# Second projection of a hybrid decoder block: copies and weight steps pinned, lag of three products, another order at its end

## The chip, the core and the metric

The kernel runs on one core of a Trainium2 chip. Its engines work in parallel, each through its own stream of instructions: TensorE (PE in the profile; its weight loads are PEld), VectorE (DVE), ScalarE (ACT), GpSimd (POOL) and SyncE (SP), from whose queue the DMA transfers leave. The metric is the device time of one execution in microseconds (us), the median of several runs.

## The reference

One decoder layer on 1024 tokens of width 1024, in float32. Two mixers read the same normalised input; each is projected, the two are merged by gates, and an output projection and a residual add follow:

```python
o_r = (head_groupnorm(o_r, ret_gn_g[l], ret_gn_b[l]) * jax.nn.silu(gr.astype(jnp.float32))).astype(x.dtype)
y = jax.nn.sigmoid(gate_a) * (o_a @ w_proj_a[l]) + jax.nn.sigmoid(gate_b) * (o_r @ w_proj_b[l])
x = x + y @ w_out[l]
xn2 = rmsnorm(x, norm2_g[l])
x = x + jnp.square(jax.nn.relu(xn2 @ w_up[l])) @ w_down[l]
```

The change concerns `o_r @ w_proj_b`, the second projection: 2048 inputs to 1024 outputs for 1024 tokens, with the gate and the sum that make `y`, up to the start of `y @ w_out`.

## The kernel before

**Arithmetic.** Every float32 operand is split into a high and a low part (`split`, L349 to L353): ScalarE copies the high part (L350), VectorE subtracts it for the low part (L353). A product of two operands is then three matmuls, high by high, high by low and low by high. The large products are also done by a seven-product scheme (Strassen in Winograd's form): a unit of 256 outputs has the products N1 to N7, and each product is 4 x 3 = 12 matmuls.

**Second projection** (from L1130). There are eight units, 0 to 3 for the first half of the inputs and 4 to 7 for the second; `order` (L1131 to L1135) lists the 56 products. Unit j runs N6, N5, N7, N4, N3, and in between N1 and N2 of unit j + 2 are run ahead; the last ten entries are of units 6 and 7 alone: N6, N5, N7 of 6, N6 of 7, N4 of 6, N5 and N7 of 7, N3 of 6, N4 and N3 of 7. Products of one unit share three banks of PSUM (`BANK`, L280): N1 and N2 add into bank a, N6, N7 and N4 into bank b, N5 and N3 into bank d. Between two of them the bank is copied out by ScalarE: after N1 (L419, negated, into bank b), after N6 (L424) and after N7 (L427). The next product of that bank may not start before its copy is done.

**Results.** N2, N7, N4 and N3 each finish a result (`result`, L1156): a block of 128 outputs by 512 tokens. For units 0 to 3 it goes to memory (`pb_d`), for half of them after being gated. For units 4 to 7 it is added up, gated by the sigmoid of a gate loaded from `sg_d`, added to the first projection's block (L1171 to L1173 or L1175 and L1176, on VectorE) and split into the rows that the output projection reads (`keep`, L1151), either at once or, for the even lower halves, after a trip through memory (`yl_d`). Each result asks for the loads of the result after next (`fetch`) and runs the sigmoid of the next one (L906). The first gate's sigmoid is run ahead of the loop (L1196).

**Weights** (`Weights`, L38). A queue of weight steps is run in order by `pump`. A unit has two raw loads of 128 x 1024 on SP and four steps: A (for N1 and N2), D (for N4), then four sums of raw blocks (L124, on VectorE), B (for N6 and N3) and C (for N5 and N7). A step needs its raw block and the release of its weight buffer (`W.free` at the end of `product`). `lag` counts how many products must lie between the request of a load and a step on it; `tick`, once a product, runs at most one step. After the 32 steps of this stage come the eight of the output projection (`add`).

**Order.** TensorE's stream is the program's order. For the other engines a planner orders the instructions by when it thinks them ready, so an instruction may move ahead of others that stand before it in the program. `tc.keep_in_program_order` ties one instruction behind the one that was traced last on its engine. Before the change the sigmoids (L906) are tied so, and the splits of the operands at the end of the stage before (`part_sum`); in this stage bank copies, weight steps and results aren't.

Of the kernel before, what the change touches and what calls it, by code (L numbers as in the profile page):

```python
# [10 lines left out]
F = mybir.dt.float32  # L11
R = mybir.dt.float32r
AF = mybir.ActivationFunctionType
OP = mybir.AluOpType
# [23 lines left out]
class Weights:  # L38
# [10 lines left out]
    A, B, C, D = (0, 1), (2, 3), 5, 4  # L49
# [24 lines left out]
            self.last[p] = key  # L74
        return before

    def add(self, src, buf=None):

        n = self.plain
        if buf is None:  # L80
            buf = self.cycle[self.turn % self.WB]
            self.turn += 1
        r = len(self.src)
        self.src.append(src)
        self.place.append(n % self.RAW)
        w = src.shape[1]

        def step():
            h, l = self.buffer(buf)
            self.split(h[:, :w], l[:, :w], self.raw[r][:, :w])  # L90
            self.units[n] = h, l
            self.used.add(r)

        self.steps.append((self.claim(buf, n), r, step))
        self.plain += 1

    def add_units(self, tag, srcs, flip=0):

        base = len(self.src)
        self.first[tag] = len(self.steps)  # L100
        kept = {}
        for s in srcs:
            self.place += [(len(self.src) + i - base) % (self.RAW + 1) for i in range(2)]
            self.src += [s[1], s[0]]

        def piece(key, buf, r, cols, then=None):
            def step():
                if isinstance(buf, tuple):
                    if not kept:
                        kept["D"] = self.buffer(buf[0])  # L110
                    h, l = (x[:, 512 * buf[1]:512 * buf[1] + 512] for x in kept["D"])
                else:
                    h, l = self.buffer(buf)
                self.split(h, l, self.raw[r][:, cols], key[0] == "up" and key[1] < 2 and key[2] != "A")
                self.units[key] = h, l
                if then:
                    then()

            self.steps.append((self.claim(buf, key), r, step))

        def sums(r):
            (x22, x21), (x11, x12) = ((self.raw[i][:, 0:512], self.raw[i][:, 512:1024]) for i in (r, r - 1))
            for x, y in ((x22, x21), (x21, x11), (x11, x22), (x12, x11)):
                ins = self.nc.vector.tensor_tensor(x, x, y, op=OP.add)  # L124
                if tag == "up" and r <= base + 3:
                    self.keep(ins)

        both = slice(0, 1024)
        for j in range(-1, len(srcs)):
            if j + 1 < len(srcs):  # L130
                piece((tag, j + 1, "A"), self.A[(j + 1) % 2], base + 2 * (j + 1), both)
            if j >= 0:
                r = base + 2 * j + 1
                piece((tag, j, "D"), (self.D, j % 2), r, slice(0, 512), lambda r=r: sums(r))
                piece((tag, j, "B"), self.B[(j + flip) % 2], r - 1, both, lambda r=r: self.used.add(r - 1))
                piece((tag, j, "C"), self.C, r, both, lambda r=r: self.used.add(r))
        m = len(srcs) + flip
        self.cycle = (0, 1, self.B[m % 2], self.C, self.D, self.B[(m - 1) % 2])
        self.turn = 0
# [90 lines left out]
class Pipe:  # L230
# [22 lines left out]
            if after:  # L253
                after(i)

    def step(self, ps, terms, ends=None, first=True):
        fns = self.due.pop(self.slot, [])
        n, m = len(terms), len(fns)
        place = {}
        for j, fn in enumerate(fns):  # L260
            place.setdefault(min(n - 1, (j + 1) * n // (m + 1)), []).append(fn)

        def after(i):
            for fn in place.get(i, []):
                fn()
            if ends and i in ends:
                ends[i]()

        self.group(ps, terms, after, first)
        self.slot += 1  # L270
        self.tick()

# [22 lines left out]
def hybrid_block(ctx: ExitStack, tc: tile.TileContext, a: dict, out: bass.AP):  # L297
    nc = tc.nc
# [47 lines left out]
    def bcast_row(src):  # L346
        return bass.AP(tensor=src.tensor, offset=src.offset, ap=[[0, P], [1, D]])

    def split(dst_h, dst_l, src, pin=False):  # L349
        hi = nc.scalar.activation(dst_h, src, AF.Copy)  # L350
        if pin:
            tc.keep_in_program_order(hi)
        nc.vector.tensor_tensor(dst_l, src, dst_h.bitcast(F), op=OP.subtract)  # L353

    half = const.tile([P, 2], F, name="half")
    nc.vector.memset(half, -0.5)
# [30 lines left out]
    W.add_units("pb", [a["w_pb_q"][j] for j in range(8)])  # L387
    for nb in range(2):
        for u in range(4):
            W.add(a["w_out"][nb, u], (4, 3, 5, 2)[u] if nb else (0, 1, 5, 2)[u])  # L390
    NU, RING = FF // 256, 10
    W.add_units("up", [a["w_up"][j] for j in range(NU)])
    NC = FF // 512
# [6 lines left out]
    def product(tag, j, name, unit, operands, pu, result):  # L400

        u = unit.setdefault(j, {})
        bank = BANK[name]
        fresh = bank not in u
        if fresh:
            u[bank] = mm.tile([P, 512], F, name="mm")
        piece, half = OPERAND[name]
        wh, wl = W[tag, j, piece]
        xh, xl = operands[name]
        terms = []  # L410
        for k in range(4):
            o = 512 * half + k * P
            terms.append((wh[:, o:o + P], wl[:, o:o + P], xh[:, k, :], xl[:, k, :]))
        pipe.step(u[bank], terms, None, fresh)
        ps = u[bank]
        lo, hi = halves()
        if name == "N1":
            u["b"] = ms.tile([P, 512], F, name="ms")
            nc.scalar.activation(u["b"], ps, AF.Copy, scale=-1.0)  # L419
        elif name == "N2":  # L420
            result(j, 0, lo, ps)
        elif name == "N6":
            u["u2"] = pu().tile([P, 512], F, name="u2")
            nc.scalar.activation(u["u2"], ps, AF.Copy)  # L424
        elif name == "N7":
            u["u3"] = pu().tile([P, 512], F, name="u3")
            nc.scalar.activation(u["u3"], ps, AF.Copy)  # L427
            nc.vector.tensor_tensor(u["u3"], u["u3"], u["d"], op=OP.subtract)
            result(j, 1, hi, u["u3"])
        elif name == "N4":  # L430
            result(j, 1, lo, ps)
        elif name == "N3":
            nc.vector.tensor_tensor(u["u2"], ps, u["u2"], op=OP.subtract)
            result(j, 0, hi, u["u2"])
        if name in ("N2", "N7", "N4", "N3"):
            W.free((tag, j, piece))
# [636 lines left out]
    with ExitStack() as ph:  # L1073
# [66 lines left out]
        def fetch(n):  # L1140

            if n >= len(results):
                return
            j, f, i = results[n]
            d, cs = 2 * (j % 4) + f, halves()[i]
            if j < 4 and f:
                return
            srcs = [sg_d[1], pa_d] if j < 4 else [sg_d[1], pb_d] + [pa_d] * f
            ahead[n] = [loaded(pm3, src[d, :, cs], "s") for src in srcs]

        def keep(j, f, cs, y):  # L1151

            yh, yl = (x[:, f, cs] for x in as_rows(YS[j - 4]))
            split(yh, yl, y)

        def result(j, f, cs, src):  # L1156

            n = results.index((j, f, cs.start // 512))
            fetch(n + 2)
            if n + 1 in ahead:  # L1160
                sigmoid(ahead[n + 1][0])
            if n not in ahead:
                y = src
                if src.space == PSUM:
                    y = pm3.tile([P, 512], F, name="s")
                    nc.scalar.activation(y, src, AF.Copy)
                nc.sync.dma_start(pb_d[2 * j + f, :, cs], y)
                return
            sgb, y, *pa = ahead.pop(n)
            if pa:  # L1170
                nc.vector.tensor_tensor(y, y, src, op=OP.add)  # L1171
                nc.vector.tensor_tensor(y, y, sgb, op=OP.mult)
                nc.vector.tensor_tensor(y, y, pa[0], op=OP.add)  # L1173
            else:
                nc.vector.tensor_tensor(sgb, sgb, src, op=OP.mult)  # L1175
                nc.vector.tensor_tensor(y, y, sgb, op=OP.add)  # L1176
            if j < 4:
                nc.sync.dma_start(pb_d[2 * j + f, :, cs], y)
            elif f or cs.start:
                keep(j, f, cs, y)  # L1180
            else:
                nc.sync.dma_start(yl_d[j - 4], y)
# [7 lines left out]
        def load_part(c, name, k):  # L1190

            return loaded(pm3, on_d[2 * c + k // 2, 2 * SUMS.index(name) + k % 2], "s")

        fetch(0)
        fetch(1)
        sigmoid(ahead[0][0])  # L1196
        for i, (j, name) in enumerate(order):
            product("pb", j, name, unit, OPB[j // 4], lambda: parts, result)
            todo += [(1, after[j, name], k) for k in range(4) if (j, name) in after]
            if (j, name) == (1, "N6"):  # L1200
                todo += [(1, "N1", k) for k in range(4)]
# [12 lines left out]
        assert not todo and not begun and not late  # L1214
        W.lag, W.pace = 0, None
        W.pump()
        e1.close()


# [410 lines left out]
```

## Time and profile before

| what | value |
|---|---|
| median of 3 runs | 2179.66 us (2179.34 to 2180.16) |
| profiled execution, its own time | 2182.39 us |
| its span in the trace | 2180.6 us |
| mean granted TensorE clock | 0.999 |
| second projection in the trace | 1305.67 to 1462.94 us |
| HBM traffic over the span | 164 GB/s |

Times of trace rows are counted from the start of the span. A timeline row gives the start, the duration, the engine, the line, the operation, what it writes and reads, a count, and in brackets the idle time before it with what ended it. Rows of a window give its bounds and length, then the busy time of PE, PEld, DVE, ACT and POOL with counts, the granted clock, the DMA share and GB/s. The chain of waits is followed back from the last instruction; its rows are start, duration and what took it.

### The profile page before, as it was taken

Reading aid. Unit: us, or ns where it says so; the run is one execution under the profiler, and the core shown is the slowest. Engines: PE = TensorE matmul, PEld = TensorE weight load, DVE = VectorE, ACT = ScalarE, POOL = GpSimd, SP = SyncE. Lnnn points to the kernel's source line nnn. Section 1 sums busy time; section 2 is a strip of 40 time slices with the busy share of each in tenths; the row PEclk is TensorE's granted clock in tenths of the full one; section 3 lists DMA queues with packets and bytes.
Section 4 is the critical chain, followed back from the end, with each engine's and each line's share of the span. In section 5 each row is a group of like instructions: output and inputs, shape, how many; then the busy total and the mean of one; then the engine's idle time right before and its main releaser. Section 6 shows DMA issues by size and latency. Waiting matters only on the chain. (4 is left out here: it accounts for less than half of the span.)

```text
span 2180.6 us, 28667 instructions
## 1 busy us (share of the span) xinstructions
PE 2155.0 (99%) x9928; PEld 1766.4 (81%) x9928; DVE 1355.3 (62%) x2327; ACT 1097.9 (50%) x2097; POOL 313.2 (14%) x340
## 2 busy tenths in 40 slices
PE   8999999999999999999999999999999999999999
PEld 6887777788888887888888877778788887888887
DVE  5723443565556665657767767783865556788884
ACT  5425555444655554545555645552654545755552
POOL 0000000000000000002123120000000000777773
PEclk9999999999999999999999999999999999999999
DMA  5323333333658676664364487774255546745443
GB/s 206 132 80 95 113 102 102 99 133 120 199 174 239 199 220 191 204 196 142 110 189 123 131 281 259 264 243 151 87 150 159 153 146 199 235 150 191 167 140 107
DMA packets 294579, 358.81 MB, mean 165 GB/s; under 512 B 35025, under 2 KB 202385, under 8 KB 294178
## 3 DMA queue, kind: packets, MB, share of 16 engines
q1 hardware_dynamic: 293890, 356.72, 52.1%
q8 instruction: 78, 1.28, 0.2%
q14 instruction: 67, 0.55, 0.1%
q10 hardware_dynamic: 544, 0.26, 0.0%
HBM read 240.33 MB, written 116.59 MB: 164 GB/s over the span
## 5 line engine op out<-in xcount | busy, mean ns | idle before, releaser
L353 DVE TENSOR_TENSOR wl<-raw,wh 128x1024 fp32r<-128x1024 f32 (+1 forms) x308 | 343.0, 1115 | 461.3 <-ACT wh L350 460.2
L350 ACT ACTIVATE wh<-raw 128x1024 fp32r<-128x1024 f32 (+1 forms) x308 | 296.2, 963 | 298.9 <-PE ms L247 106.9
L247 PE MATMUL mm<-xh,wh 128*128 128x512 f32 x960 | 388.2, 404 | 1.1 <-ACT ms L419 1.0
L247 PE MATMUL mm<-xh,wl 128*128 128x512 f32 x960 | 375.5, 391 | 0.0
L247 PE MATMUL mm<-xl,wh 128*128 128x512 f32 x960 | 374.6, 390 | 0.9 <-DVE xl L353 0.9
L247 PE MATMUL ms<-xh,wh 128*128 128x512 f32 x784 | 319.3, 407 | 7.4 <-ACT u L427 3.7
L247 PE MATMUL ms<-xh,wl 128*128 128x512 f32 x784 | 307.2, 392 | 0.8 <-DVE wl L353 0.8
L247 PE MATMUL ms<-xl,wh 128*128 128x512 f32 x784 | 306.5, 391 | 0.0
L247 PEld LDWEIGHTS mm<-xh,wl 128*128 128x128 f32 x960 | 180.3, 188 | 39.3 <-DVE wl L353 0.6
L247 PEld LDWEIGHTS mm<-xh,wh 128*128 128x128 f32 x960 | 180.6, 188 | 36.1 <-ACT ms L419 1.9
L247 PEld LDWEIGHTS mm<-xl,wh 128*128 128x128 f32 x960 | 180.9, 188 | 35.2 <-DVE xl L353 1.3
L247 PEld LDWEIGHTS ms<-xh,wh 128*128 128x128 f32 x784 | 147.9, 189 | 48.9 <-issue 10.1
L247 PE MATMUL mm<-wh,xh 128*128 128x512 f32 x458 | 186.3, 407 | 0.3 <-ACT xh L350 0.3
L247 PE MATMUL mm<-wh,xl 128*128 128x512 f32 x458 | 179.8, 393 | 0.9 <-DVE xl L353 0.9
L996 POOL TENSOR_TENSOR st<-st,half 128x1 f32<-128x1 f32 x32 | 25.5, 796 | 1076.3 <-DVE st L995 1076.3
L247 PE MATMUL mm<-wl,xh 128*128 128x512 f32 x458 | 178.8, 390 | 0.0
L247 PEld LDWEIGHTS ms<-xh,wl 128*128 128x128 f32 x784 | 147.6, 188 | 33.1 <-DVE wl L353 1.2
L247 PEld LDWEIGHTS ms<-xl,wh 128*128 128x128 f32 x784 | 148.2, 189 | 27.1
L247 PEld LDWEIGHTS mm<-wh,xl 128*128 128x128 f32 x458 | 86.0, 188 | 20.6 <-DVE xl L353 1.4
L247 PEld LDWEIGHTS mm<-wh,xh 128*128 128x128 f32 x458 | 86.3, 188 | 16.3 <-ACT xh L350 0.8
L247 PEld LDWEIGHTS mm<-wl,xh 128*128 128x128 f32 x458 | 86.6, 189 | 15.6
L247 PE MATMUL ms<-wh,xh 128*128 128x512 f32 x232 | 92.5, 399 | 0.0
(309 smaller groups left out, 3824.2 us busy)
## 6 DMA issues: line engine op xcount, KB each, us to landing
raw<-in_w_up SPq DMA_DIRECT2D x32, 512.0 KB, 3.9
h_d<-s SPq DMA_DIRECT2D x64, 256.0 KB, 4.3
raw<-in_w_down SPq DMA_DIRECT2D x32, 512.0 KB, 3.8
raw<-in_w_aqk_q SPq DMA_DIRECT2D x24, 512.0 KB, 3.5
qk_d<-sg SPq DMA_DIRECT2D x48, 256.0 KB, 3.0
qk<-qk_d SPq DMA_DIRECT2D x24, 512.0 KB, 6.8
rb<-rs_d SPq DMA_DIRECT2D x24, 512.0 KB, 7.3
xh<-h_d SPq DMA_DIRECT2D x11, 896.0 KB, 4.7
```

The source lines that it names most:

```text
L247: self.nc.tensor.matmul(ps, x, y, start=start, stop=stop, skip_group_check=not first)
L350: hi = nc.scalar.activation(dst_h, src, AF.Copy)
L353: nc.vector.tensor_tensor(dst_l, src, dst_h.bitcast(F), op=OP.subtract)
L996: nc.gpsimd.tensor_tensor(st[:, 9:10], st[:, 8:9], half[:, 0:1], op=OP.pow)
```

## The change

Six edits, all within the second projection and its weight steps:

- The copies after N1, N6 and N7 are tied in program order, in this stage only.
- `tick` is called after the product with its copy and result, where it used to be called inside the product's matmuls; `W.lag` is set to 3 (it was 2 from the stage before).
- The weight steps of units 2 to 7 (both halves of the split) and their sums are tied in program order; so are both halves of the splits of the output projection's first four weight blocks.
- The three VectorE operations of the next to last result, (7,N4), and both halves of its split are tied in program order.
- The splits of (6,N7), (7,N7) and (6,N3) are put off into a list, `last`, and so is the whole result of (7,N3).
- The list is run after the stage's last `W.pump()`.

```diff
@@ Weights.add @@
-            self.split(h[:, :w], l[:, :w], self.raw[r][:, :w])
+            self.split(h[:, :w], l[:, :w], self.raw[r][:, :w], pin, pin)
@@ Weights.add_units @@
-                self.split(h, l, self.raw[r][:, cols], key[0] == "up" and key[1] < 2 and key[2] != "A")
+                late = key[0] == "pb" and key[1] > 1
+                self.split(h, l, self.raw[r][:, cols], late or key[0] == "up" and key[1] < 2 and key[2] != "A", late)
...
-                if tag == "up" and r <= base + 3:
+                if tag == "pb" and r > base + 4 or tag == "up" and r <= base + 3:
                     self.keep(ins)
@@ Pipe.step @@
         self.slot += 1
-        self.tick()
+        if tick:
+            self.tick()
@@ split @@
-        nc.vector.tensor_tensor(dst_l, src, dst_h.bitcast(F), op=OP.subtract)
+        lo = nc.vector.tensor_tensor(dst_l, src, dst_h.bitcast(F), op=OP.subtract)
+        if both:
+            tc.keep_in_program_order(lo)
@@ weights of the output projection @@
-            W.add(a["w_out"][nb, u], (4, 3, 5, 2)[u] if nb else (0, 1, 5, 2)[u])
+            W.add(a["w_out"][nb, u], (4, 3, 5, 2)[u] if nb else (0, 1, 5, 2)[u], not nb)
@@ product @@
-        pipe.step(u[bank], terms, None, fresh)
+        pipe.step(u[bank], terms, None, fresh, tag != "pb")
+        keep = tc.keep_in_program_order if tag == "pb" else lambda ins: None
...
-            nc.scalar.activation(u["b"], ps, AF.Copy, scale=-1.0)
+            keep(nc.scalar.activation(u["b"], ps, AF.Copy, scale=-1.0))
...
-            nc.scalar.activation(u["u2"], ps, AF.Copy)
+            keep(nc.scalar.activation(u["u2"], ps, AF.Copy))
...
-            nc.scalar.activation(u["u3"], ps, AF.Copy)
+            keep(nc.scalar.activation(u["u3"], ps, AF.Copy))
@@ keep and result of the second projection @@
-        def keep(j, f, cs, y):
+        last, done = [], []
+
+        def keep(j, f, cs, y, pin=False):
...
-            split(yh, yl, y)
+            split(yh, yl, y, pin, pin)
...
+            if n == len(results) - 1 and n in ahead and not done:
+                done.append(n)
+                last.append(lambda: result(j, f, cs, src))
+                return
...
-                nc.vector.tensor_tensor(y, y, src, op=OP.add)
-                nc.vector.tensor_tensor(y, y, sgb, op=OP.mult)
-                nc.vector.tensor_tensor(y, y, pa[0], op=OP.add)
+                for with_, op in ((src, OP.add), (sgb, OP.mult), (pa[0], OP.add)):
+                    ins = nc.vector.tensor_tensor(y, y, with_, op=op)
+                    if n == len(results) - 2:
+                        tc.keep_in_program_order(ins)
+                if n == len(results) - 2:
+                    return keep(j, f, cs, y, True)
...
+            elif j > 5 and cs.start and n < len(results) - 1:
+                last.append(lambda: keep(j, f, cs, y))
@@ the loop over the products @@
+        W.lag = 3
         fetch(0)
         fetch(1)
         sigmoid(ahead[0][0])
         for i, (j, name) in enumerate(order):
             product("pb", j, name, unit, OPB[j // 4], lambda: parts, result)
+            pipe.tick()
...
         W.lag, W.pace = 0, None
         W.pump()
+        for fn in last:
+            fn()
         e1.close()
```

More of the change, by code (lines that the diff above doesn't have):

```diff
@@ L75, in claim, with add @@
         return before
-    def add(self, src, buf=None):
+    def add(self, src, buf=None, pin=False):
         n = self.plain
@@ L254, in group, with step @@
                 after(i)
-    def step(self, ps, terms, ends=None, first=True):
+    def step(self, ps, terms, ends=None, first=True, tick=True):
         fns = self.due.pop(self.slot, [])
@@ L347, in bcast_row, with split @@
         return bass.AP(tensor=src.tensor, offset=src.offset, ap=[[0, P], [1, D]])
-    def split(dst_h, dst_l, src, pin=False):
+    def split(dst_h, dst_l, src, pin=False, both=False):
         hi = nc.scalar.activation(dst_h, src, AF.Copy)
```

## The prediction

> **What bounds the kernel now.** I read the head of the page first, then one window over the second projection and the first product of the output projection, then TensorE's waits in that window, then the timelines of each engine around each wait. Products are counted from 1305.67 us, twelve matmuls each; (3,N7) is product N7 of unit 3.
>
> ```profile
> span 2180.6 us, 28667 instructions
> ...
> PE 2155.0 (99%) x9928; PEld 1766.4 (81%) x9928; DVE 1355.3 (62%) x2327; ACT 1097.9 (50%) x2097; POOL 313.2 (14%) x340
> ```
>
> ```profile
> 1305.67:1470.21 164.54, 160.07 (x697) 130.11 (x696) 133.42 (x188) 87.21 (x135) 0.00 (x0) 1.00 0.77 255
> ```
>
> ```profile
> 1418.44 5.44 PE mm L247 x24
> ```
>
> The second line of the page says that TensorE is the bound: 99% of the span. So the change can only gain what TensorE loses in its own stretch. The chain of waits gives the pace when nothing is missing: 24 matmuls in 5.44 us, 2.72 us a product. The stretch holds 56 products of the projection and two products' worth of the output projection's first row tile: 58 x 2.72 = 157.8 us. It took 164.54 us (windows view: length, then busy times of PE, PEld, DVE, ACT and POOL, clock, DMA share, GB/s). **The loss is 6.8 us, 0.31% of the run, and that is the ceiling of the gain.** Where it lies:
>
> ```profile
> PE ms L247 <- ACT u L427: 2.2, 3, 1.0
> PE mm L247 <- DVE xl L353: 0.9, 1, 0.9
> PE ms L247 <- DVE wl L353: 0.8, 1, 0.8
> PE mm L247 <- ACT xh L350: 0.3, 1, 0.3
> PE mm L247 <- ACT ms L419: 0.2, 1, 0.2
> ```
>
> ```profile
> 1311.47 0.50 PE L247 MATMUL mm<-xh,wh 128*128 128x512 f32 x1 [0.20 <-ACT ms L419]
> ...
> 1331.77 0.50 PE L247 MATMUL ms<-xh,wh 128*128 128x512 f32 x1 [0.96 <-ACT u L427]
> ```
>
> The listed idle is 4.4 us; each wait costs about 0.3 us more than its bracket, because a matmul is shown 0.39 us long and starts every 0.23 us, and the first after a wait is slow; a seventh wait is too short to be listed. By starts, (0,N2) loses 0.5 us at 1311.47 and the other six places 6.3 us.
>
> **Part 1: bank copies and weight steps in program order.** What makes the copy of an N7 bank (L427) late is this:
>
> ```profile
> 1323.10 0.58 ACT L419 ACTIVATE ms<-mm 128x512 f32<-128x512 f32 x1
> 1328.71 1.06 ACT L350 ACTIVATE wh<-raw 128x1024 fp32r<-128x1024 f32 x1 [5.03 <-DMA raw<-in_w_pb_q]
> ...
> 1330.20 1.04 ACT L350 ACTIVATE wh<-raw 128x1024 fp32r<-128x1024 f32 x1
> 1331.15 0.57 ACT L427 ACTIVATE u<-ms 128x512 f32<-128x512 f32 x1
> ```
>
> ```profile
> 1322.94 5.75 DMA raw<-in_w_pb_q
> ```
>
> ScalarE stands 5.03 us before piece A of unit 3, whose load left at 1322.94, while the bank of (0,N7) is full at about 1328.2. In the code that split stands behind this copy; the planner put it ahead. With the copy pinned, and A pinned behind it, the copy runs at 1328.2 and (0,N4) starts in time. The same holds for (1,N4), (2,N4) and (4,N4). Lag 3 and the moved tick change little by themselves: the tick now stands behind the product's copy, but also behind its release of a weight buffer, so a step that waits for a buffer lands between the same two copies as before. By that count the splits keep their place among the copies, and their loads (512 KB on SP) pass only the loads of retention sums and late rows issued in the same round; both are asked three products, 8.2 us, before their split, against 5.75 us of transit, so I cost this at nothing. If that cover fails, a late load holds ScalarE, and with it the next pinned copy, by the difference.
>
> **What the pins hold back at the start.** Pinning ties an instruction behind the one traced last on its engine. Ahead of the copy of (0,N1) that is the sigmoid of the first gate, which stands before the loop.
>
> ```profile
> 1309.88 1.06 ACT L350 ACTIVATE xh<-oraw 128x1024 fp32r<-128x1024 f32 x1 [0.23 <-DMA oraw<-on_d]
> 1310.84 1.06 ACT L419 ACTIVATE ms<-mm 128x512 f32<-128x512 f32 x2
> ...
> 1317.58 0.63 ACT L906 ACTIVATE s<-s 128x512 f32<-128x512 f32 x1 [1.25 <-DMA s<-sg_d]
> ```
>
> ```profile
> 1310.28 1.23 DVE xl L353
> ...
> 1311.52 5.97 DMA s<-sg_d
> ```
>
> Today both N1 copies (x2) run at 1310.84, ahead of the sigmoid at 1317.58. Afterwards the first may not. The sigmoid waits for a gate load that leaves SP at 1311.52, when VectorE's last but one split of the stage before has given its memory back, and travels 5.97 us; nothing in the change moves that. So the copy ends at 1317.58 + 0.63 + 0.58 = 1318.8 in place of about 1311.4. (0,N2) adds to that same bank and has nothing ahead of it to run: it starts at 1318.8 in place of 1311.47, **+7.3 us**. Behind the held copy on ScalarE stand the splits of A(2) and B(1), needed three and more products later; TensorE is the one that waits. Bounds: if VectorE freed the memory right when the split's input is there, 0.6 us sooner, 6.7; 7.6 with the handshakes.
>
> **Clock after that wait.**
>
> ```profile
> 1290.30 0.50 PE L247 MATMUL ms<-xh,wh 128*128 128x512 f32 x1 [1.97 <-DVE s L1099]
> ```
>
> ```profile
> 1290.00:1295.00 5.00, 4.70 (x14) 3.71 (x15) 2.76 (x4) 1.74 (x3) 0.00 (x0) 0.66 1.05 400
> ```
>
> After the one long wait near here, 1.97 us, the granted clock of the next 5 us is 0.66: 0.34 x 5 = 1.7 us lost. A wait of 7.3 us should cost at least about as much: **+1.7 us**, bounds 0.8 (half as much, if the slowing starts early in the wait and ends soon) and 3.4 (twice). [...]
>
> **What the pins hold back late.** A B split needs the four sums of its unit (L124); it is now pinned ahead of the next N6 copy (L424), and itself behind the row split of the N3 result, which needs L1176. In units up to 5 an N6 copy has two products between (N1, N5) before N7 adds to its bank; (6,N6) has only N5.
>
> ```profile
> 1437.63 0.58 ACT L424 ACTIVATE u<-ms 128x512 f32<-128x512 f32 x1
> 1440.70 1.06 ACT L350 ACTIVATE wh<-raw 128x1024 fp32r<-128x1024 f32 x1 [2.49 <-DVE raw L124]
> ```
>
> ```profile
> 1439.98 0.68 DVE L124 TENSOR_TENSOR raw<-raw 128x512 f32<-128x512 f32 x1
> 1440.59 0.68 DVE L1176 TENSOR_TENSOR s<-s 128x512 f32<-128x512 f32 x1
> ```
>
> ```profile
> 1440.04 0.39 PE L247 MATMUL ms<-xh,wh 128*128 128x512 f32 x1
> ```
>
> ```profile
> 1434.60:1462.94 28.34, 27.52 (x122) 22.47 (x120) 25.05 (x36) 14.42 (x23) 0.00 (x0) 1.00 0.75 249
> ```
>
> Today the copy of (6,N6) runs at 1437.63, three microseconds ahead of the split of B(7), and (6,N7) starts at 1440.04. With the sums where they are, the split ends at 1441.8 and the copy at 1442.3: 2.3 us late. With the row split between (1440.59 + 0.68, then 0.63, 1.06, 0.58) it is 1443.5: 3.5 us late. VectorE is full here (25.05 of 28.34 us in the windows view), so I don't expect the sums much earlier: **+2.8 us**, bounds 0 (sums pinned in one run of 2.4 us and done 3 us sooner) and 4. For unit 5:
>
> ```profile
> 1423.46 1.06 ACT L350 ACTIVATE wh<-raw 128x1024 fp32r<-128x1024 f32 x1
> ```
>
> ```profile
> 1423.72 0.39 PE L247 MATMUL ms<-xh,wh 128*128 128x512 f32 x1
> ```
>
> B(6) at 1423.46 would put the copy of (5,N6) at 1425.1 and (5,N7) 1.4 us late, 2.2 with the earlier loss at (4,N4) gone. But there VectorE was late because L427 was; its work starts some 2.5 us sooner afterwards. **+0.7 us**, bounds 0 and 2.2.
>
> **Part 2: the end.** The output projection's eighth k block needs the split of (7,N4).
>
> ```profile
> 1463.86 0.68 DVE L1171 TENSOR_TENSOR s<-s,ms 128x512 f32<-128x512 f32 x1
> 1464.46 1.22 DVE L353 TENSOR_TENSOR wl<-raw,wh 128x1024 fp32r<-128x1024 f32 x1
> ...
> 1469.13 0.68 DVE L353 TENSOR_TENSOR xl<-s,xh 128x512 fp32r<-128x512 f32 x1
> ```
>
> From L1171 to the end of that split are 5.9 us, with two weight splits, an L433 and an L1175 in between; pinned in one run it is 3 x 0.7 + 0.63 + 0.7 = 3.4 us, and it starts earlier, because three row splits and the last result's work stand behind it now. By the count of starts (7,N4) ends near 1460.2; VectorE is free of what stays ahead within a microsecond, so the split is done near 1464.7; TensorE needs it 7.5 us after (7,N4), at 1467.7 (12 + 21 matmuls). The two waits go, 1.8 of the 6.3 us. What is put off, six VectorE and four ScalarE instructions of about 0.6 us, is hidden: it feeds row tiles 4 to 7, four row tiles (21.8 us) later, and without that cover costs about 4 us. The wait on wl (1.1 us) at (7,N6) falls into the new wait ahead of (6,N7).
>
> **Sum**: +7.3 + 1.7 + 2.8 + 0.7 - 6.3 = +6.2 us. The profiled execution, 2182.39 us with what lies around its span, becomes 2188.6. It stands 2.7 us over the median of the runs, 2179.66, so the median becomes 2185.9.
>
> **Rivals.** (a) *Only the start is held.* If the sums come early enough, late units lose nothing: 7.3 + 1.7 - 6.3 = +2.7 us, 2182.4. For it: the pins also take VectorE's idle times away. Against: VectorE is full from 1430 on. (b) *The start is not held*: the gate load gets onto SP some 6 us sooner, or the copy does not truly stand behind the sigmoid. Then late waits stay: 3.5 - 6.3 = -2.8 us, 2176.9. Against: that load's memory is free only at 1311.5. (c) *Neither is held*, the stretch runs without a wait: -6.8 us, 2172.9. This is the faster side; its place is the six waits, and it decides as soon as the first N1 copy ends before 1311.1 and the copy of (6,N6) before 1440. (d) *The pins change nothing that counts*, since the planner finds the same order: 2179.7. Against: the rows at 1310.84 and 1437.63 are in an order that the pins forbid.
>
> **Chances.** Forecast 0.60, (a) 0.20, (b) 0.08, (c) 0.09, (d) 0.03. A measurement can tell about 0.2%, 4.4 us, from no change. Slower by more: 0.54 of the forecast and 0.05 of (a), 0.59. Faster by more: 0.08 of (c) and 0.01 of (b), 0.09. The rest, 0.32, lies within. The likeliest case by its bounds runs from 2182 to 2191; to leave out no more than 2 in 10 the range reaches down into (b): 2177 to 2191.
>
> **What would show it.** Right: a wait of 7 us of TensorE on L419 right after (1,N1), the sigmoid just ahead of that copy, a clock well under 1 after it; no wait on L427; a wait on L424 ahead of (6,N7); none at the start of the output projection. Wrong: the first N1 copy before the first sigmoid, or a gate load that leaves SP before 1306 us; waits on L427 that stay; a stretch of under 160 us.

## The result and the profile after

The changed kernel takes 2196.25 us (median of six runs, 2195.06 to 2197.32) beside 2179.91 us of the kernel before on the same chip: a ratio of 1.0075, 95% interval 1.0065 to 1.0085. It is **slower by 16 us** (14 to 19 by the interval). The prediction was 2185.9 us with a range up to 2191: the sign was right, the size was not.

The profiled execution took 2196.76 us. Its span is 2195.0 us, where it was 2180.6. The windows view of the stretch from the first matmul of the second projection to the same matmul of the output projection as before (columns as explained above):

```profile
1305.57:1485.19 179.62, 164.25 (x698) 133.65 (x696) 134.43 (x187) 88.88 (x136) 0.00 (x0) 0.96 0.70 234
```

The stretch took 179.62 us in place of 164.54, 15.1 us more; the span grew by 14.4 us. So the whole loss lies in the second projection. Against the 157.8 us of 58 products without a wait it is 21.8 us, where it was 6.8.

TensorE's waits inside the stretch (who waited for whom, us in total, times, longest):

```profile
PE ms L248 <- ACT u L429: 7.6, 2, 4.1
PE mm L248 <- ACT ms L424: 7.5, 1, 7.5
PE ms L248 <- ACT u L432: 0.2, 1, 0.2
```

L248, L424, L429 and L432 are the lines 247, 419, 424 and 427 of before; below, too, the same line moves by a few numbers from kernel to kernel. The six old waits are gone but for 0.2 us on an N7 copy (L432); none is listed at the start of the output projection. In their place stand three waits on copies that the change has tied: one on the first N1 copy (L424), two on N6 copies (L429).

**The first wait**, ahead of (0,N2). The chain of waits (start, duration, what took it):

```profile
1311.17 1.23 DVE xl L355
...
1312.42 4.96 DMA s<-sg_d
...
1317.47 0.63 ACT s L911
1318.10 0.49 ACT ms L424
...
1318.64 3.78 PE mm L248 x8
```

It is the chain that the prediction wrote down, item by item: VectorE's split frees the memory, the gate load travels 5 us, the sigmoid, the copy tied behind it, TensorE. The eight matmuls behind it take 3.78 us; eight at the full pace of 0.23 us take 1.8.

**The two late waits.** ScalarE's timeline ahead of (5,N7) and (6,N7):

```profile
1432.84 1.06 ACT L352 ACTIVATE wh<-raw 128x1024 fp32r<-128x1024 f32 x1 [3.14 <-DVE raw L125]
1433.80 0.58 ACT L429 ACTIVATE u<-ms 128x512 f32<-128x512 f32 x1
...
1454.55 1.06 ACT L352 ACTIVATE wh<-raw 128x1024 fp32r<-128x1024 f32 x1 [3.78 <-DVE raw L125]
1455.52 0.58 ACT L429 ACTIVATE u<-ms 128x512 f32<-128x512 f32 x1
```

TensorE's timeline at the same places:

```profile
1429.92 0.39 PE L248 MATMUL mm<-xh,wl 128*128 128x512 f32 x1
1434.43 0.50 PE L248 MATMUL ms<-xh,wh 128*128 128x512 f32 x1 [4.13 <-ACT u L429]
...
1452.26 0.39 PE L248 MATMUL mm<-xh,wl 128*128 128x512 f32 x1
1456.15 0.79 PE L248 MATMUL ms<-xh,wh 128*128 128x512 f32 x1 [3.50 <-ACT u L429]
```

Both times ScalarE stands idle for over 3 us in front of a weight split (B of the next unit) whose sums (L125) aren't there, with the copy that TensorE needs tied behind it.

**The clock** after each of the three waits, by windows of 5 us:

```profile
1318.60:1323.60 5.00, 4.96 (x14) 3.97 (x15) 3.13 (x5) 4.60 (x8) 0.00 (x0) 0.60 0.97 343
1434.40:1439.40 5.00, 4.96 (x15) 3.94 (x16) 0.76 (x1) 0.78 (x2) 0.00 (x0) 0.66 0.28 105
1456.10:1461.10 5.00, 4.95 (x16) 4.02 (x17) 0.77 (x1) 0.56 (x2) 0.00 (x0) 0.70 0.32 105
```

The granted clocks 0.60, 0.66 and 0.70 cost 2.0, 1.7 and 1.5 us. With 0.3 us beside each bracket (as in the prediction) the three places add up to 7.8 + 2.0, 4.4 + 1.7 and 3.8 + 1.5 = 21.2 us, of the 21.8 that the stretch lost.

### The profile page after: what moved, and what is told of

Its sections match the earlier page's. It is cut to its first block, busy times and chain, and to the rows that moved or that the text cites. A ratio compares the mean times of both kernels' runs of the same rounds, so it can differ in the third digit from the quotient of the medians.

```text
span 2195.0 us, 28654 instructions
## 1 busy us (share of the span) xinstructions
PE 2157.1 (98%) x9928; PEld 1767.4 (81%) x9928; DVE 1356.8 (62%) x2327; ACT 1100.6 (50%) x2097; POOL 313.8 (14%) x340
## 4 chain that ended last, share of the span: by engine, by line
PE 81%; DVE 5%; DMA 5%; issue 3%; ACT 3%; POOL 2%; SPq 0%; POOLq 0%; DVEq 0%; ACTq 0%
PE mm L248 41%; PE ms L248 34%; PE tr L689 1%; PE tr L668 1%; DMA s<-on_d 1%; DVE wl L355 1%; ACT wh L352 1%; DVE xl L355 1%; ACT xh L352 1%; PE tr L679 1%; DMA pa_d<-s 1%; PE tr L818 1%; PE tr L1028 1%; PE ms L968 1%; DMA s<-sg_d 0%
## 5 line engine op out<-in xcount | busy, mean ns | idle before, releaser
L248 PE MATMUL mm<-xh,wh 128*128 128x512 f32 x960 | 388.5, 405 | 8.3 <-ACT ms L424 8.3
L248 PE MATMUL mm<-xl,wh 128*128 128x512 f32 x960 | 374.9, 391 | 0.9 <-DVE xl L355 0.9
L248 PE MATMUL mm<-xh,wl 128*128 128x512 f32 x960 | 375.6, 391 | 0.0
L248 PE MATMUL ms<-xh,wh 128*128 128x512 f32 x784 | 319.5, 407 | 11.8 <-ACT u L429 8.8
L248 PE MATMUL ms<-xh,wl 128*128 128x512 f32 x784 | 307.1, 392 | 0.0
L248 PE MATMUL ms<-xl,wh 128*128 128x512 f32 x784 | 306.7, 391 | 0.0
L248 PEld LDWEIGHTS mm<-xh,wh 128*128 128x128 f32 x960 | 181.0, 189 | 44.0 <-ACT ms L424 9.3
L248 PEld LDWEIGHTS mm<-xh,wl 128*128 128x128 f32 x960 | 180.6, 188 | 39.5 <-DVE wl L355 0.7
L248 PEld LDWEIGHTS mm<-xl,wh 128*128 128x128 f32 x960 | 181.1, 189 | 35.5 <-DVE xl L355 1.3
L248 PEld LDWEIGHTS ms<-xh,wh 128*128 128x128 f32 x784 | 148.0, 189 | 53.4 <-ACT u L429 10.1
L248 PE MATMUL mm<-wh,xh 128*128 128x512 f32 x458 | 186.0, 406 | 0.0
L248 PE MATMUL mm<-wh,xl 128*128 128x512 f32 x458 | 179.5, 392 | 0.1
L248 PE MATMUL mm<-wl,xh 128*128 128x512 f32 x458 | 178.4, 390 | 0.0
L248 PEld LDWEIGHTS ms<-xh,wl 128*128 128x128 f32 x784 | 147.9, 189 | 31.9
L248 PEld LDWEIGHTS ms<-xl,wh 128*128 128x128 f32 x784 | 148.4, 189 | 27.2
L248 PEld LDWEIGHTS mm<-wh,xl 128*128 128x128 f32 x458 | 85.9, 188 | 19.7 <-DVE xl L355 0.5
L248 PEld LDWEIGHTS mm<-wl,xh 128*128 128x128 f32 x458 | 86.5, 189 | 15.6
L248 PEld LDWEIGHTS mm<-wh,xh 128*128 128x128 f32 x458 | 86.2, 188 | 15.6 <-ACT ms L1466 0.3
L248 PE MATMUL ms<-wh,xl 128*128 128x512 f32 x232 | 91.1, 393 | 1.6 <-DVE ss L370 1.6
```

What stands on the lines that cost most here:

```text
L248: self.nc.tensor.matmul(ps, x, y, start=start, stop=stop, skip_group_check=not first)
```

## The experiments

Each is timed against the kernel before on the same chip. Times of one kernel scatter (the kernel before took 2176.44 to 2185.39 us in 27 executions on one chip), so the ratios with their 95% intervals carry the comparison, and the traces say where the time went. Everything is computed in each of them; only the order is another.

**The two causes, one at a time and together.** Three kernels take the ties away from the copies on which the changed kernel waits.

Run e1_first_copy_free:

```diff
-            keep(nc.scalar.activation(u["b"], ps, AF.Copy, scale=-1.0))
+            (keep if j else lambda ins: None)(nc.scalar.activation(u["b"], ps, AF.Copy, scale=-1.0))
```

> The kernel after, with one tie taken away: the copy after N1 of unit 0 is no longer tied in program order (all else as after). Theory (the tie behind the first gate's sigmoid holds that copy): the 7.6 us wait of TensorE at (0,N2) and the slow clock after it (1.25 us in the trace of after) go, so 2196.25 - 8.9 = 2187.4 us, and both N1 copies stand ahead of the first sigmoid in ScalarE's stream. Rival (the later tick and the lag of 3 make the loads at the start late, whatever is tied): the wait stays, 2196 us.

Run e2_n6_copies_free:

```diff
-            keep(nc.scalar.activation(u["u2"], ps, AF.Copy))
+            (keep if j < 5 else lambda ins: None)(nc.scalar.activation(u["u2"], ps, AF.Copy))
```

> The kernel after, with the copies after N6 of units 5, 6 and 7 no longer tied. Theory (they stand behind the split of B of the next unit, and that behind the four sums): the waits ahead of (5,N7) and (6,N7), 4.3 and 3.7 us, go, and with them the slow clock after each, about 1.7 us: 2196.25 - 11.4 = 2184.9 us. Rival (VectorE is the bound there, and the wait only moves on to the low half of B of unit 7 at (7,N6)): about half comes back, 2188 to 2192 us.

Run e3_both_free, both edits:

> The kernel after with both of these ties taken away. Theory: the two effects add up, 2196.25 - 8.9 - 11.4 = 2176 us, faster than before by about 4 us, since the other gains of the change are left (no waits on the copies after N7, none at the start of the output projection). Rival (the change has no gain, only these losses): 2179.9 us, the same as before.

| kernel | median, us | ratio to before, interval | difference |
|---|---|---|---|
| after | 2196.25 | 1.0075, 1.0065 to 1.0085 | +16.3 |
| e1: first N1 copy untied | 2191.29 | 1.0046, 1.0032 to 1.0059 | +10.0 |
| e2: N6 copies of units 5 to 7 untied | 2188.78 | 1.0034, 1.0023 to 1.0046 | +7.4 |
| e3: both | 2181.01 | 0.9999, 0.999 to 1.0008 | -0.2 |

(Differences: ratio less 1, times 2180 us.) The start is worth 6.3 us by e1 and 7.6 from e2 to e3; the late copies 8.9 us by e2 and 10.2 from e1 to e3. Together they are the whole 16 us. So by the medians **the late units hold the larger part, not the start**, the reverse of the prediction's sum (9.0 for the start with its clock, 3.5 for the late units); the trace above says the same (11.4 us there, 9.8 at the start), while the intervals of e1 and e2 overlap. Neither e1 nor e2 gave back what its theory asked for (2187.4 and 2184.9 us; for the clock at the start the theory of e1 took 1.25 us, where the window above gives 2.0). For e2 the rival held: the wait partly moved on to (7,N6), where TensorE now waits 1.3 us for the high half of B(7) and 0.5 us for its low half, with a granted clock of 0.66 over the 5 us from there. TensorE's waits in the stretch, e3:

```profile
PE mm L248 <- ACT ms L424: 1.5, 1, 1.5
PE ms L248 <- ACT u L432: 1.0, 2, 0.6
PE ms L248 <- ACT wh L352: 0.8, 1, 0.8
PE ms L248 <- DVE wl L355: 0.5, 1, 0.5
PE mm L248 <- DVE wl L355: 0.4, 1, 0.4
```

No long wait is left, and yet e3 is no faster than the kernel before: 4.2 us of short waits, as many as before (4.4), only elsewhere. My theory that the six old waits would then show as a gain fell, the rival held. One of the new places is seen best in e1, in the timeline of ScalarE and in the waits of TensorE:

```profile
1317.35 0.63 ACT L911 ACTIVATE s<-s 128x512 f32<-128x512 f32 x1 [4.72 <-DMA s<-sg_d]
...
1318.83 0.61 ACT L911 ACTIVATE s<-s 128x512 f32<-128x512 f32 x1
1319.35 1.04 ACT L352 ACTIVATE wh<-raw 128x1024 fp32r<-128x1024 f32 x1
```

```profile
PE mm L248 <- ACT ms L424: 1.7, 1, 1.7
PE mm L248 <- DVE wl L355: 1.2, 1, 1.2
```

The split at 1319.35 is A(2). It is now tied behind both late sigmoids, and (2,N1) waits 1.2 us for its low half; untied (run e5, below) it runs at 1314.99, when its load has landed. The prediction had counted this split as needed "three and more products later" and free, which it was only as long as TensorE itself was held. At (0,N2), though its copy is free, 1.7 us are left; that isn't the work of the tie, since e5 (1.5 us) and e10 (1.4 us), where both copies run ahead of the sigmoid, have as much. So e1 gains less than the first place had lost.

**Which tie makes the start late.** Run e5_first_tie_alone puts only the tie of that one copy into the kernel before:

```diff
-            nc.scalar.activation(u["b"], ps, AF.Copy, scale=-1.0)
+            ins = nc.scalar.activation(u["b"], ps, AF.Copy, scale=-1.0)
+            if tag == "pb" and j == 0:
+                tc.keep_in_program_order(ins)
```

> The kernel before with one tie added and no other edit: the copy after N1 of unit 0 is tied in program order. Theory (that tie alone makes the wait at the start): TensorE waits 7 to 8 us at (0,N2), the clock after it costs 1.2 to 1.7 us, in all 8 to 9 us slower than before; that taking the tie away from the changed kernel gave 5 us only is then because other ties of that kernel leave waits of their own at the start. Rival (the tie is worth 5 us whatever stands around it): 5 us slower.

A miss: 2181.33 us, ratio 1.0007 (0.9998 to 1.0016). The copies run ahead of the sigmoid, as they did before:

```profile
1310.73 1.06 ACT L419 ACTIVATE ms<-mm 128x512 f32<-128x512 f32 x2
1314.99 1.06 ACT L350 ACTIVATE wh<-raw 128x1024 fp32r<-128x1024 f32 x1 [3.20 <-DMA raw<-in_w_pb_q]
1316.97 0.63 ACT L908 ACTIVATE s<-s 128x512 f32<-128x512 f32 x1 [0.92 <-DMA s<-sg_d]
```

The reason I found in the code: with the tick inside the product, a weight split (C of unit 0) is traced between the sigmoid and the copy. The tie binds the copy behind that split alone, and the split, untied, may run early. Run e7_lag_and_tick_alone is the other half, lag 3 and the moved tick without any tie:

```diff
-        self.tick()
+        if tick:
+            self.tick()
...
+        W.lag = 3
...
             product("pb", j, name, unit, OPB[j // 4], lambda: parts, result)
+            pipe.tick()
```

> The kernel before with the lag of 3 and the tick behind the product alone, nothing tied. Theory: the splits keep their places among the copies, no wait of TensorE goes or comes: as before, within 1 us. Rival (the later lag moves the loads and with them the waits on the copies after N7): the four waits on those copies change by more than 1 us in sum.

In the time nothing, as expected: 2181.67 us, ratio 1.0001 (0.9992 to 1.001). In its trace the rival's sign is there: the waits on N7 copies come to 0.7 us in place of 2.2, and others are longer. What that is worth can't be told from one trace: they come to 1.5 us in e5, whose one tie stands elsewhere. Run e9_tick_and_first_tie has both halves and nothing else:

> The kernel before, with lag 3, the moved tick and the tie of the first N1 copy together, nothing else. Theory: with the tick behind the product the copy stands directly behind the first gate's sigmoid in the trace of the program, so the tie now binds: TensorE waits 7 to 8 us ahead of (0,N2) and loses about 1.3 us more to the clock; 8 us over the kernel before, about 2188. Rival (each of the two alone did nothing, so neither do both): within 2 us of the kernel before.

2187.89 us, ratio 1.0033 (1.0022 to 1.0043): 7 us slower. The profiled execution was the longest of its eight, 2191.66 us. Of ScalarE, of TensorE and of the window behind the wait:

```profile
1319.93 0.63 ACT L909 ACTIVATE s<-s 128x512 f32<-128x512 f32 x1 [6.17 <-DMA s<-sg_d]
1320.46 1.06 ACT L420 ACTIVATE ms<-mm 128x512 f32<-128x512 f32 x2
```

```profile
1321.10 0.80 PE L247 MATMUL mm<-xh,wh 128*128 128x512 f32 x1 [8.33 <-ACT ms L420]
```

```profile
1321.10:1326.10 5.00, 5.00 (x12) 3.94 (x13) 3.03 (x4) 4.10 (x7) 0.00 (x0) 0.50 0.85 293
```

**Two edits that each do nothing that can be measured cost 7 us together**: the moved tick brings the copy directly behind the sigmoid, and only then does the tie bind to it.

**What holds the N6 copies.** Run e6_d_b_sums_free leaves the copies tied and unties what stands ahead of them, the D and B splits and the sums:

```diff
-                late = key[0] == "pb" and key[1] > 1
+                late = key[0] == "pb" and key[1] > 1 and key[2] in "AC"
...
-                if tag == "pb" and r > base + 4 or tag == "up" and r <= base + 3:
+                if tag == "up" and r <= base + 3:
```

> The kernel after, with the steps D and B and the four sums between them untied (A, C and all copies stay tied). Theory (the sums of units 6 and 7 come late because they are tied behind D, and D behind the row split of the result before, so that the copies after N6 come late): the sums move up, the waits ahead of (5,N7) and (6,N7), 4.3 and 3.7 us, shrink to under 2.5 us each, the clock stays up, and the run is 4 to 7 us shorter: 2189 to 2192 us. Rival (VectorE is full there, and the order of the sums on it doesn't matter): both waits stay within 1 us, 2196 us.

2190.82 us, ratio 1.0048 (1.0034 to 1.0062), inside the expected 2189 to 2192. The long wait at the start stays, the two on L429 shrink from 7.6 to 4.1 us in total:

```profile
PE ms L248 <- ACT u L429: 4.1, 2, 2.3
```

ScalarE ahead of (6,N7) in that kernel:

```profile
1453.11 0.63 ACT L352 ACTIVATE xh<-s 128x512 fp32r<-128x512 f32 x1 [3.58 <-DVE s L1190]
...
1454.73 0.58 ACT L429 ACTIVATE u<-ms 128x512 f32<-128x512 f32 x1
```

So nearly half of these waits is the tied weight work; the copy still comes behind the row split of a result that VectorE finishes late. That is the tie of the copy, which e2 takes away.

**The parts meant to gain, alone.** Run e4_end_alone is the kernel before with the three edits at the end (the next to last result tied, the others put off into the list):

```diff
+            if n == len(results) - 1 and n in ahead and not done:
+                done.append(n)
+                last.append(lambda: result(j, f, cs, src))
+                return
...
+                if n == len(results) - 2:
+                    return keep(j, f, cs, y, True)
...
+            elif j > 5 and cs.start and n < len(results) - 1:
+                last.append(lambda: keep(j, f, cs, y))
...
+        for fn in last:
+            fn()
```

> The kernel before with the change's end alone: the operations and the split of (7,N4) tied in program order, the splits of (6,N7), (7,N7), (6,N3) and the result of (7,N3) put behind the last pump; no other edit. Theory: the two waits at the start of the output projection go, 1.8 us: 2178.1 us. Rival (the four row splits put off are late for something else, or the weight splits still come first): 2180 us.

In its trace the two waits at the output projection's start are gone, as the prediction said. In the time it can't be told from nothing: 2180.13 us, ratio 0.9996 (0.9987 to 1.0005), an interval from -2.8 to +1.1 us that holds the expected gain and zero.

Run e8_n7_and_a_c_tied is the kernel before with the N7 copies tied and the high halves of A and C from unit 2 on:

```diff
+                late = key[0] == "pb" and key[1] > 1 and key[2] in "AC"
-                self.split(h, l, self.raw[r][:, cols], key[0] == "up" and key[1] < 2 and key[2] != "A")
+                self.split(h, l, self.raw[r][:, cols], late or key[0] == "up" and key[1] < 2 and key[2] != "A")
...
-            nc.scalar.activation(u["u3"], ps, AF.Copy)
+            ins = nc.scalar.activation(u["u3"], ps, AF.Copy)
+            if tag == "pb":
+                tc.keep_in_program_order(ins)
```

> The kernel before with the copies after N7 tied, and the high halves of the splits A and C of units 2 to 7, nothing else. Theory (the N7 copies come late only behind a split A whose load is late): the waits ahead of the N4 products go, about 3 us, and no new wait comes: 2177 to 2178 us beside 2180.4. Rival (the copies then wait behind row splits and sigmoids whose loads are late): the waits stay or move, no gain.

A miss: 2185.12 us, ratio 1.0018 (1.0009 to 1.0027). The N7 waits fell to 0.7 us, but A(2) was tied behind the sigmoid, as in e1, and the wait ahead of (7,N6) grew (the first row, 0.8 us before) and slowed the clock (0.66 granted over the 5 us behind it):

```profile
PE ms L248 <- DVE wl L354: 1.6, 1, 1.6
...
PE mm L248 <- DVE wl L354: 1.4, 2, 1.2
```

**A version without the harmful ties.** Run e10_n7_a_and_end is the changed kernel without the ties that were shown to hold something and those of their kind: N1 and N6 copies, D, B and C, the sums and A(2) (of C, and of the other N1 and N6 copies, no run shows that they held anything). What stays is the tie of the N7 copies, of A from unit 3 on, of the four weight splits of the output projection, lag, tick and end:

```diff
-                late = key[0] == "pb" and key[1] > 1
+                late = key[0] == "pb" and key[1] > 2 and key[2] == "A"
...
-                if tag == "pb" and r > base + 4 or tag == "up" and r <= base + 3:
+                if tag == "up" and r <= base + 3:
...
-            keep(nc.scalar.activation(u["b"], ps, AF.Copy, scale=-1.0))
+            nc.scalar.activation(u["b"], ps, AF.Copy, scale=-1.0)
...
-            keep(nc.scalar.activation(u["u2"], ps, AF.Copy))
+            nc.scalar.activation(u["u2"], ps, AF.Copy)
```

> The kernel after, with the copies after N1 and N6, the D, B and C steps, the sums and A of unit 2 untied; what stays is the tie of the N7 copies, of A from unit 3 on, of the output projection's first weight splits, lag 3, the moved tick and the end. Theory: nothing held at the start or late, waits on N7 copies gone, the two at the start of the output projection gone: 3 to 4 us under the kernel before, about 2176. Rival (the ties that stay move the waits to other products, as before): within 1.5 us of the kernel before.

2176.12 us, ratio 0.9975 (0.9965 to 0.9986): **faster than both**, by 4.6 us of the medians against the kernel before (3 to 8 by the interval). Its stretch and all its waits there:

```profile
1304.64:1465.20 160.56, 158.74 (x697) 130.35 (x696) 133.18 (x187) 88.76 (x136) 0.00 (x0) 1.00 0.79 262
```

```profile
PE mm L248 <- ACT ms L424: 1.4, 1, 1.4
PE mm L248 <- DVE xl L355: 0.3, 1, 0.3
```

160.56 us against 164.54: 4.0 us won, of a ceiling of 6.8. TensorE no longer waits for an N7 copy in this trace; at the output projection 0.3 us is left (the second row), where it was 1.2.

Two variants: e11_n7_a_end_w_free unties the weight splits of the output projection and the low half of A, and e12_n7_a_end_old_tick has besides that lag 2 and the tick in its old place.

```diff
-                self.split(h, l, self.raw[r][:, cols], late or key[0] == "up" and key[1] < 2 and key[2] != "A", late)
+                self.split(h, l, self.raw[r][:, cols], late or key[0] == "up" and key[1] < 2 and key[2] != "A")
...
-            W.add(a["w_out"][nb, u], (4, 3, 5, 2)[u] if nb else (0, 1, 5, 2)[u], not nb)
+            W.add(a["w_out"][nb, u], (4, 3, 5, 2)[u] if nb else (0, 1, 5, 2)[u])
```

> As the one before, with the output projection's weight splits untied and the low half of A untied too. Theory: if the tied weight splits cause the waits of 0.9 to 1.2 us at (7,N6), these go: about 1 to 2 us under the one before. Rival (VectorE's load in the last units causes them): the waits stay, no difference.

> As the one before, with lag 2 and the tick inside the product, as in the kernel before. Theory: the planner's order decides, not the tick, so it is within 1.5 us of the one before. Rival: a step that stands behind the copy in the program lets the N7 tie bind to something else, and waits of 0.8 to 1 us on N7 copies come back: 2 to 3 us over the one before.

2178.49 us, ratio 0.9985 (0.9976 to 0.9994), and 2177.16 us, ratio 0.9984 (0.9975 to 0.9992). The waits ahead of (7,N6) were absent in e10, with the tied splits, and 0.6 us are there in both variants without them (e11):

```profile
PE ms L248 <- DVE wl L355: 0.6, 1, 0.6
```

In e11 there are besides 2.6 us of waits on N7 copies:

```profile
PE ms L248 <- ACT u L432: 2.6, 3, 1.7
```

So the theory for e11 has the wrong sign: these ties help if anything. For e12 the theory held, the tick's place isn't what decides. The three intervals overlap; which of the three is best stays open, and so does which edit of e10 brings its gain. That it is the tie of the N7 copies isn't shown: with that tie the waits on them run from none (e10) to 2.6 us (e11), without it from 0.4 us (e9) to 2.2 (before), one trace each, and the end alone (e4) gained nothing that can be measured.

## Why the prediction was wrong, and where it was right

By its own steps, in the profiled executions (the measured values are bracket + 0.3 us and the clock windows above):

| step of the sum | predicted | measured |
|---|---|---|
| (0,N2) behind the first gate's sigmoid | +7.3 | 7.8, less 0.5 lost there before: +7.3 |
| clock after that wait | +1.7 | +2.0 |
| (6,N7) behind the split of B(7) | +2.8 | 3.8, and 1.5 of clock: +5.3 |
| (5,N7) behind the split of B(6) | +0.7 | 4.4, and 1.7 of clock: +6.1 |
| the six waits go | -6.3 | -5.8 (0.5 left over, by the listed waits) |
| sum | +6.2 | +14.9 (stretch: +15.1) |

Of the 8.7 us between the sums, 3.7 are the wait at (5,N7), 3.2 the clock after the two late waits, 1.0 the wait at (6,N7) and 0.8 the rest.

- **Right:** the first wait to a tenth of a microsecond (in part by luck: the gate load left 0.9 us later than before, 1312.42 for 1311.52, which "nothing in the change moves", and travelled 1.0 us less, 4.96 for 5.97), the chain behind it, the clock after it within its bounds, the end of the waits on N7 copies, a wait ahead of (6,N7) on its N6 copy, no waits at the output projection. Rivals (a) to (d) all fell as a whole.
- **The step that failed is (5,N7), +0.7.** The prediction read 1.4 us of wait from the rows of before, let TensorE come 0.8 us sooner (2.2 us), and took 1.5 us off again, because VectorE's "work starts some 2.5 us sooner afterwards". What has to be compared is the time behind the first wait and its clock, where everything stands 9.0 us later than before ((0,N6) starts at 1326.02 for 1317.05). TensorE got to (5,N7) at 1430.15 us (1429.92 + 0.23); its old start, 1423.72, moved by 9.0 us gives 1432.7, so it was 2.5 us sooner, since TensorE lost that much less ahead of the N4 products. The split of B(6) ran at 1432.84; its old place, 1423.46, moved by 9.0 us gives 1432.4, so it was 0.4 us *later*. The new wait is the sum: 1.4 us from the rows, 2.5 from TensorE, 0.4 from B(6), 4.3 us. The gain of the one part became the wait of the other.
- **VectorE did start sooner; the tied sums did not follow.** VectorE before, from the subtraction behind the copy of (4,N7) to the first and the last of the four sums that B(6) needs:

```profile
1410.19 0.68 DVE L428 TENSOR_TENSOR u<-u,mm 128x512 f32<-128x512 f32 x1
...
1418.54 0.68 DVE L124 TENSOR_TENSOR raw<-raw 128x512 f32<-128x512 f32 x1
...
1422.75 0.68 DVE L124 TENSOR_TENSOR raw<-raw 128x512 f32<-128x512 f32 x1
```

After, first VectorE, then ScalarE:

```profile
1416.39 0.69 DVE L433 TENSOR_TENSOR u<-u,mm 128x512 f32<-128x512 f32 x1 [0.66 <-ACT u L432]
...
1428.26 0.69 DVE L355 TENSOR_TENSOR wl<-raw,wh 128x512 fp32r<-128x512 f32 x1
1428.98 0.69 DVE L125 TENSOR_TENSOR raw<-raw 128x512 f32<-128x512 f32 x1
...
1432.12 0.69 DVE L125 TENSOR_TENSOR raw<-raw 128x512 f32<-128x512 f32 x1
```

```profile
1426.98 0.64 ACT L352 ACTIVATE xh<-s 128x512 fp32r<-128x512 f32 x1 [4.29 <-DVE s L1183]
1427.52 0.62 ACT L352 ACTIVATE wh<-raw 128x512 fp32r<-128x512 f32 x1
```

Against the shift of 9.0 us the subtraction is 2.8 us sooner, as the prediction said, but the first sum is 1.4 us later and the last 0.4. The sums are now tied behind the low half of D(6) (1428.26), whose high half (1427.52) is tied behind the row split of (4,N4)'s result (1426.98), and that waits 4.29 us for VectorE itself. Before, sums ran in between the operations of the results. In e6, where D, B and the sums are untied, they do follow: there everything behind the first wait stands 13.8 us later than before ((0,N6) at 1330.85), and the last sum comes 3.0 us sooner than that; the wait ahead of (5,N7) is 1.7 us in place of 4.1:

```profile
1433.60 0.69 DVE L125 TENSOR_TENSOR raw<-raw 128x512 f32<-128x512 f32 x1
```

- **The second step: the clock was charged to one wait of three.** The prediction took its own row of 1.97 us of idle time as enough to slow the clock, and forecast waits of 2.8 us at (6,N7), yet charged nothing there. The two late waits, of 3.5 and 4.1 us, cost 3.2 us of clock.
- (6,N7) alone, 3.8 us for +2.8, lay above the upper of the two readings (2.3 and 3.5 us) between which the prediction chose, and within its bounds.
- "Lag 3 and the moved tick change little by themselves" is borne out by e7 in the time, but the sum had no term for what they do together with the tie. That didn't harm the number, since the tie was judged in the kernel with both.
- The two long waits were the larger error, but not the only thing that ate the gain: without them (e3) the kernel comes out even. Rival (c), neither held and 2172.9 us, asked too much of the remaining ties; taking more of them away (e10) brought 4 us of the 6.8.

## What to carry to other kernels

A tie in program order is a dependency on whatever is traced just before it: write down that predecessor and its inputs for each tied instruction, above all loads in flight and work of a full engine, since the tie turns their lateness into the wait of the engine behind. Tie only what was shown to be overtaken, not everything around it (the kernels here that came out faster, e10 to e12, tie the N7 copies and the A splits from unit 3 on, and none of the steps D, B and C), and judge a tie in the final order of the code, since moving a neighbour can change what it binds to. When a part of a change makes the bounding engine faster, move its time forward before you cost the next wait, and follow each producer up to the operation that is waited for: here VectorE started sooner, and the tied sums that counted didn't.

## What the runs showed of the hardware

In these traces no one length of a wait divides those with a slow TensorE clock behind them from those without. The waits of 3.50 us and more shown above all had one: over the 5 us behind it, 0.70 after 3.50 us, 0.50 after 8.33 us (e9). Of the shorter ones some did and most did not. Counted by the starts of matmuls between 1240 and 1600 us in the fourteen traces, three of 32 gaps of 1.4 to 2.7 us were followed by slow matmuls (some 0.43 us from start to start for 0.23), and all eight of 3.8 us and more. In the kernel before 1.97 us gave 0.66 (shown with the prediction, which so built on the rarer case). In e6 the wait ahead of (6,N7), 2.32 us, was longer and cost no clock (1.00); TensorE's timeline and the window behind it:

```profile
1455.36 0.50 PE L248 MATMUL ms<-xh,wh 128*128 128x512 f32 x1 [2.32 <-ACT u L429]
```

```profile
1455.30:1460.30 5.00, 4.94 (x22) 4.06 (x22) 1.96 (x3) 1.85 (x4) 0.00 (x0) 1.00 0.51 158
```

The waits of 7.5 and 8.33 us cost 2.0 and 2.5 us of clock by their windows, the one of 1.97 us in the kernel before 1.7 us, and the one of 2.32 us none. What decides whether a wait has a slow clock behind it, no run here shows.
